# Sixteen of 22 feed-forward blocks go through the down projection as two chunks with seven products for eight

## The chip, the cores and the metric

The kernel runs on one core of one Trainium2 chip. Its engines each work through a list of instructions of their own, in order: TensorE (PE) multiplies matrices, with a separate entry PEld for its weight loads; VectorE (DVE) and ScalarE (ACT) do elementwise work; GpSimd (POOL) does a little of it; SyncE (SP) mostly issues DMA transfers between memory and the chip. An instruction that waits for another engine or for a transfer holds up everything behind it on its own engine. The metric is the device time of one execution in microseconds (us). Three runs of the kernel before gave 2496.0, 2497.52 and 2500.09 us, so the median is 2497.52 us.

## What is computed

One inference step of a hybrid decoder with one trunk layer, for a prompt of 1024 tokens and a group of 8 single-token samples, 1032 columns in all. Three token mixers (a gated convolution, a state-space scan, an attention over 256 memory tokens) read one combined input projection `w_in`; their merged output is added to `x`; then comes the feed-forward:

```python
def swiglu(xn, w_gate, w_up, w_down):
    return (jax.nn.silu(xn @ w_gate) * (xn @ w_up)) @ w_down
...
xp = xp + h
xp = xp + swiglu(rmsnorm(xp, norm_ffn_w[l]), w_ffn_gate[l], w_ffn_up[l], w_ffn_down[l])
```

`D_MODEL` is 1024 and the hidden width is 2816, so there are 22 hidden blocks of 128 (`NF`). A final RMSNorm follows. Everything is float32, and the outputs include the states of the mixers (`state_ssm` among them).

## The kernel before, in words

**Products.** Activations lie transposed, 128 features on the partitions and the 1032 tokens (`TT`) along the row. Each float32 operand is split into a high and a low part by a cast on ACT (`h`) and a subtraction on DVE (`l`), and each product is made of three: high by high, high by low, low by high.

**Plain and seven-for-eight products.** `gemm` (L194) multiplies eight or fewer blocks plainly; for a block of 128 output features and one of 128 input features it makes three matrix multiplications of 1032 columns, each issued as 256, 512 and 264 columns. `strassen` (L298) computes two output blocks from eight input blocks. It sees weights and activations as 2x2 matrices and makes seven products of half size where the plain way needs eight. The activation side of a product, its form, is a sum of token halves and feature halves: `B11`, `T1`, `nT2`, `B21`, `T3`, `B22`, `T4`. Each product runs over four pairs of 128 features with 516 columns (`HT`, issued as 256 and 260). For the weights two raw tiles are loaded (`st_raw`, L235), summed on DVE (`sa` at L323 and L324, `sb` in `st_adds2` at L289 and L290) and split into `A`, `S`, `T` and `D` tiles (`st_split`, L243 the ACT cast, L244 the DVE subtraction). Outputs are collected from three PSUM tiles in turn (`m0`, `m1`, `m2`): the first product of each quarter by an ACT copy (L326, L334, L337), the later ones by DVE additions and subtractions. The same function serves the input projection, where the blocks `Z`, `X`, `C`, `G` and `B` go through it (the first such row is at 102.71 us), and gate and up of the feed-forward (`g0` ... `g20`, `u0` ... `u20`).

**What else runs beside it.** While the input projection runs, the samples' state recurrence is interleaved with it: a tile `st` of states is loaded by SP (L831), scaled on ACT (L839), updated and read on DVE (L841, L845) and stored by SP (L853). The four `C` pairs `C0`, `C2`, `C4`, `C6` have such ACT instructions among their own casts and copies. No order is written by hand for single instructions: a scheduler lays out each engine's list when the kernel is built, from the program's order, its buffers and its dependencies; `tick` runs small pending pieces of other work between products.

**Feed-forward.** For each pair of blocks, `hidden_pair` (L1781) runs `g` and then `u`; SiLU on ACT and three multiplications on DVE (L1809, L1810, L1811) make the hidden blocks `g..o`, and SP writes them to `h_d` (L1812, L1813). After all 22 blocks the PSUM pool of `strassen` is closed and the down projection runs with `gemm` in groups of blocks 0 to 2, 3 to 10 and 11 to 18 (`down`, L1837), each added by DVE into the eight output tiles `x3_0` ... `x3_7` (L1852), which first hold the residual read from `x2_d` (L1857). `hidden` reads blocks back (`hr`, L1823) and splits them (L172, L173). Blocks 19 to 21 go through the last loop (L1913 to L1915) together with the final normalization.

## Time and profile before

| what | value |
|---|---|
| runs shown | 2496.0, 2497.52, 2500.09 us |
| the profiled execution's own time | 2499.52 us |
| its span | 2497.8 us |
| granted TensorE clock over the span | 0.995 |
| PE busy | 2446.6 us (98%) |
| DVE busy | 1504.3 us (60%) |
| ACT busy | 1047.6 us (42%) |
| DMA | 392.08 MB, mean 157 GB/s |

The profile was taken from one execution; 1.7 us of its time lie outside the span. "Busy" counts time in which an engine has an instruction in work, so PE at 98% is an engine that hardly ever waits, not one at its peak. In a row of the timeline the first two columns are start and duration in us, then engine, source line, operation, output and inputs, with the number of instructions it groups; a bracket at the end gives the idle time before it and what ended it. The names SPq and ACTq stand for the engine's DMA issues. In a table of windows each engine's busy time in the stretch stands with the number of its instructions, then the granted clock, the DMA share and the bytes per second.

### The profile page before, as it was taken

How to read it: one execution, taken by the hardware profiler on the slowest of the kernel's cores; microseconds unless marked ns; L12 is line 12 of the kernel's file. 1: busy time of each engine (PE TensorE's matmuls, PEld its weight loads, DVE VectorE, ACT ScalarE, POOL GpSimd, SP SyncE). 2: the span in 40 equal slices, each digit the busy share in tenths (PEclk: the TensorE clock that was granted, in tenths of full speed). 3: DMA queues.
4: the chain of work that ended last, by engine and by line, in shares of the span. 5: the costliest groups of instructions: out<-in, count | busy, mean ns of one | idle time of the engine just before them, and what ended most of it. 6: DMA issues, size and time to landing. Idle time of an engine off the chain costs nothing.

```text
span 2497.8 us, 44833 instructions
## 1 busy us (share of the span) xinstructions
PE 2446.6 (98%) x18714; PEld 2313.1 (93%) x18714; DVE 1504.3 (60%) x2466; ACT 1047.6 (42%) x1688; POOL 118.4 (5%) x163
## 2 busy tenths in 40 slices
PE   7999999999999999999999989999999999999998
PEld 5899999999999999888888877899999999999998
DVE  6744587777677774656767552555775545552325
ACT  6554455353545535457445441223443333341212
POOL 0200000000000001121120000000000000000000
PEclk9999999999999999999999999999999999999999
DMA  6345434344344456667868677855443222282211
GB/s 200 105 140 162 131 103 153 111 129 128 109 136 136 130 159 216 200 206 266 268 196 274 214 271 240 265 197 170 141 153 102 93 70 85 84 278 88 68 35 69
DMA packets 348330, 392.08 MB, mean 157 GB/s; under 512 B 15334, under 2 KB 285782, under 8 KB 348119
## 3 DMA queue, kind: packets, MB, share of 16 engines
q1 hardware_dynamic: 327678, 331.50, 42.4%
q10 hardware_dynamic: 20449, 57.71, 6.0%
q8 instruction: 147, 2.41, 0.4%
q14 instruction: 56, 0.46, 0.1%
HBM read 280.40 MB, written 108.98 MB: 156 GB/s over the span
## 4 chain that ended last, share of the span: by engine, by line
PE 90%; DMA 5%; DVE 3%; ACT 2%; issue 1%; SPq 0%; ACTq 0%; POOL 0%; DVEq 0%
PE po L214 12%; PE pd L214 9%; PE ps_q L214 4%; PE pm L1710 4%; PE ps_g L214 1%; PE py L953 1%; PE pss L966 1%; PE po L945 1%; PE Z4m L256 1%; PE C3m L256 1%; PE G18m L256 1%; PE B6m L256 1%; PE X14m L256 1%; PE B4m L256 1%; PE G10m L256 1%
## 5 line engine op out<-in xcount | busy, mean ns | idle before, releaser
L1852 DVE TENSOR_TENSOR x<-pd,x 128x1032 f32<-128x1032 f32 x24 | 29.5, 1231 | 128.8 <-PE pd L214 128.8
L898 ACT ACTIVATE r<-r,acum 128x128 f32<-128x128 f32 x256 | 79.3, 393 | 3.6 <-DMA r<-ac_d 3.1
L669 DVE SCALAR_TENSOR_TENSOR ax<-u,prm,ax 128x1024 f32<-128x1024 f32 x44 | 56.3, 1281 | 0.0
L930 POOL TENSOR_TENSOR xdd<-xdt,decst 128x512 f32<-128x512 f32 x32 | 38.9, 1215 | 290.0 <-DVE xdt L926 290.0
L839 ACT ACTIVATE st<-st,es 128x128 f32<-128x128 f32 x128 | 41.6, 394 | 22.4 <-DMA st<-in_state_ssm_dram 22.4
L1357 DVE TENSOR_TENSOR yr<-po,yr 128x1032 f32<-128x1032 f32 x8 | 9.8, 1231 | 56.0 <-PE po L214 45.1
L949 DVE TENSOR_TENSOR y<-po,ea 128x512 f32<-128x512 f32 x28 | 19.3, 689 | 37.2 <-PE po L945 37.2
L924 DVE TENSOR_TENSOR r<-r,cbm 128x1024 f32<-128x1024 f32 x32 | 39.2, 1225 | 2.7 <-ACT bT L923 0.5
L841 DVE SCALAR_TENSOR_TENSOR st<-sr,dts,st 128x128 f32<-128x128 f32 x128 | 40.5, 348 | 0.4
L923 ACT COPY bT<-bp 128x128 f32<-128x128 f32 x32 | 8.5, 265 | 69.9 <-DVE cbm L921 69.8
L845 DVE SCALAR_TENSOR_TENSOR sr<-st,sr 128x128 f32<-128x128 f32 x128 | 35.5, 287 | 1.1
L953 PE MATMUL py<-r,xdt 128*64 128x128 f32 x512 | 35.0, 279 | 0.0
L899 ACT ACTIVATE r<-r 128x1024 f32<-128x1024 f32 x32 | 33.9, 1058 | 0.6
L966 PE MATMUL pss<-xdd,bT 128*128 128x512 f32 x64 | 33.4, 603 | 0.0
L926 DVE TENSOR_TENSOR xdt<-xp,dtT 128x512 f32<-128x512 f32 x32 | 21.9, 685 | 18.6 <-PE xp L919 18.4
L1717 DVE TENSOR_TENSOR x<-pm,xT 128x516 f32<-128x516 f32 x16 | 11.1, 696 | 35.1 <-PE pm L1710 35.1
L953 PEld LDWEIGHTS py<-r,xdt 128*64 128x64 f32 x512 | 27.3, 137 | 4.1 <-issue 0.5
L945 PE MATMUL po<-bc,s 128*128 128x128 f32 x224 | 29.8, 276 | 1.0 <-DVE s L972 1.0
L979 POOL TENSOR_TENSOR s<-s,cdec 128x512 f32<-128x512 f32 x28 | 30.2, 1078 | 7.4 <-DVE s L972 7.0
L945 PEld LDWEIGHTS po<-bc,s 128*128 128x128 f32 x224 | 27.6, 191 | 2.8 <-issue 1.6
L1090 DVE SCALAR_TENSOR_TENSOR x<-x,prm,sqa 128x1032 f32<-128x1032 f32 x16 | 19.7, 1288 | 14.5 <-ACT sqa L1086 14.5
L672 DVE SCALAR_TENSOR_TENSOR ax<-u,prm,ax 128x1032 f32<-128x1032 f32 x22 | 28.3, 1288 | 0.0
(9105 smaller groups left out, 8780.1 us busy)
## 6 DMA issues: line engine op xcount, KB each, us to landing
r<-ac_d SPq DMA_DIRECT2D x32, 512.0 KB
gt<-gt_d SPq DMA_DIRECT2D x24, 516.0 KB
xs_d<-ax ACTq DMA_DIRECT2D x22, 516.0 KB
hr<-h_d SPq DMA_DIRECT2D x22, 516.0 KB
gt_d<-G ACTq DMA_DIRECT2D x20, 516.0 KB
x<-xs_d SPq DMA_DIRECT2D x16, 516.0 KB
zs<-zs_d SPq DMA_DIRECT2D x16, 516.0 KB
yb_d<-x SPq DMA_DIRECT2D x16, 516.0 KB
```

The lines of the kernel that those rows point to most:

```text
L214: PE.matmul(out[:, c : c + n], wt[:, ks], x[:, c : c + n], start=(k == 0 and i == 0), stop=(k == nk - 1 and i == 2),)
L256: PE.matmul(hv(ps)[:, c : c + n], wt[:, ks], x[:, c : c + n], start=(start and kt == 0 and i == 0), stop=(kt == 3 and i == 2), skip_group_ ...
L669: V.scalar_tensor_tensor(acc[:, :T], u[:, j : j + T], w[j], acc[:, :T], op0=ALU.mult, op1=ALU.add)
L839: S.activation(st[:, i], st[:, i], AF.Copy, scale=es[:, g * 4 + i, b : b + 1])
L841: V.scalar_tensor_tensor(st[:, i], rb, dts[:, g * 4 + i, b : b + 1], st[:, i], op0=ALU.mult, op1=ALU.add)
L898: S.activation(r[:, j, :], r[:, j, :], AF.Relu, scale=-1.0, bias=acum[:, c, h : h + 1])
L924: V.tensor_tensor(r, r, bc(cbm.unsqueeze(1), [P, HPG, P]), op=ALU.mult)
L930: G.tensor_tensor(b3(xdd, HPG), b3(xdt, HPG), bc(decst[:, c, hs].unsqueeze(2), [P, HPG, 64]), op=ALU.mult)
L945: PE.matmul(po[:, t * P : (t + 1) * P], state["s"][:, t * P : (t + 1) * P], bcg[1][:, cs], start=True, stop=True,)
L953: PE.matmul(py[hp : hp + 64, (h // 2) * P : (h // 2 + 1) * P], xdt[:, h * 64 : (h + 1) * 64], r[:, (h % 2) * 4 + h // 2, :], start=True, s ...
L966: PE.matmul(pss, bT, xdd, start=True, stop=True)
L1710: PE.matmul(hv(ps)[:, c : c + n], wt[:, ks], x[:, half * HT + c : half * HT + c + n], start=(k == 0 and i == 0), stop=(k == KD - 1 and i = ...
```

## The change

Hidden blocks 0 to 15 are handled in two chunks of eight. When a pair of them is ready, four more DVE operations make its share of the seven forms in float32, and SP writes seven half-width pieces to a new array `hf_d` in place of two whole blocks. After gate and up the down projection runs four `strassen` calls over chunk 0 (`d00`, `d02`, `d04`, `d06`) and four over chunk 1 (`d10` ... `d16`), each for two output blocks, with `into=True`: the first product of each quarter is added into `x3` on DVE where an ACT copy stood. The forms' SBUF tiles are those that held the forms of gate and up: `refill` calls `h_form` after a form's last product in `u20`, which loads two tiles of that form of chunk 0 and splits them on ACT and DVE; `d06` does the same for chunk 1. Blocks 16 to 18 stay with `gemm`, blocks 19 to 21 with the last loop.

In `strassen` itself, for every caller, the second weight sum is now written over the first raw tile `raw1`, and no tile `sb` is allotted.

```diff
     def st_raw(src, name):
         raw = wp.tile([P, 1024], F32, tag="raw", name=name)
+        if len(src.shape) == 4:
+            for t in range(2):
+                in_turn("raw", SY.dma_start(raw[:, t * 512 : (t + 1) * 512].rearrange("p (k c) -> p k c", k=4), src[:, t]))
+            return raw
...
-    def st_adds2(raw1, raw2, sa, nm, sums):
-        sb = sums(f"{nm}sb")
-        V.tensor_add(sb[:, :512], raw1[:, :512], raw2[:, :512])
+    def st_adds2(raw1, raw2, sa):
+        V.tensor_add(raw1[:, :512], raw1[:, :512], raw2[:, :512])
         V.scalar_tensor_tensor(
-            sb[:, 512:], sa[:, 512:], -1.0, raw1[:, 512:], op0=ALU.mult, op1=ALU.subtract
+            raw1[:, 512:], sa[:, 512:], -1.0, raw1[:, 512:], op0=ALU.mult, op1=ALU.subtract
         )
-        return sb
+        return raw1
...
+        def first(dst, ps):
+            if into:
+                V.tensor_tensor(dst, ps, dst, op=ALU.add)
+            else:
+                S.copy(dst, ps)
+        def used(f):
+            if refill is not None:
+                refill(f)
...
-            S.copy(o11, hv(pa))
+            first(o11, hv(pa))
+            used("B11")
...
+    def h_form(ch, f):
+        for i in range(2):
+            t = ev_tile(f"hf{ch}{f}{i}", (P, 2 * HT))
+            SY.dma_start(t, hf_d[ch, FORMS.index(f), i])
+            mk = fx.get(f) or act_pair
+            hi, lo = mk("ah", f"h{ch}{f}{i}h"), mk("al", f"h{ch}{f}{i}l")
+            split_to(hi, lo, t.rearrange("p (a c) -> p a c", a=2))
+            hforms[ch][f] += [(hi[:, a], lo[:, a]) for a in range(2)]
...
-        u1, u2, pa = hidden_pair("u", j)
+        u1, u2, pa = hidden_pair("u", j, (lambda f: h_form(0, f)) if j == NF - 2 else None)
...
-        SY.dma_start(h_d[j], s1)
-        SY.dma_start(h_d[j + 1], s2)
+        if j >= 16:
+            SY.dma_start(h_d[j - 16], s1)
+            SY.dma_start(h_d[j - 15], s2)
+            continue
+        b11, b12, b21, b22 = (t[:, c] for t in (s1, s2) for c in HS)
+        t1, t3, nt2, t4 = (t[:, c] for t in (u1, u2) for c in HS)
+        V.tensor_sub(t1, b12, b11)
+        V.tensor_sub(t3, b22, b12)
+        V.tensor_sub(nt2, t1, b22)
+        V.scalar_tensor_tensor(t4, nt2, -1.0, b21, op0=ALU.mult, op1=ALU.subtract)
+        kt = (j % 8) // 2
+        for f, t in enumerate((b11, t1, nt2, b21, t3, b22, t4)):
+            SY.dma_start(hf_d[j // 8, f, kt // 2][:, (kt % 2) * HT : (kt % 2 + 1) * HT], t)
...
+    for ch in range(2):
+        for m in range(0, KD, 2):
+            strassen(
+                w_rows(ch, m), w_rows(ch, m + 1), hforms[ch], f"d{ch}{m}", ev_sums,
+                lambda m=m: (x2[m][:, HS[0]], x2[m][:, HS[1]], x2[m + 1][:, HS[0]], x2[m + 1][:, HS[1]]),
+                into=True, refill=(lambda f: h_form(1, f)) if ch == 0 and m == KD - 2 else None,
+            )
...
-    js = [0, 1, 2]
-    for nxt in (range(3, 11), range(11, 19), range(19, 22)):
-        down(js, [hs.pop(j) for j in js])
-        js = list(nxt)
-        for j in js:
-            hs[j] = hidden(j)
+    js = [16, 17, 18]
+    down(js, [hs.pop(j) for j in js])
+    js = [19, 20, 21]
+    for j in js:
+        hs[j] = hidden(j)
```

The new listing shifts lines: L390 is the subtraction in `split_to` that makes a form's low part, L1850 to L1852 are the three multiplications of the pair, L248 and L247 are the two halves of `st_split`, L340 and L341 make `sa`, L293 and L294 the sum in place, L311 the ACT copy in `first`, L381 the new last subtraction into `x3`, L867 the scaling of `st`.

First place, DVE at the end of the last up pair `u20`. Before, the list holds the multiplications of the pair between splits of weights (`wd..l`) and blocks (`h..l`) for the plain down projection:

```order
L350 TENSOR_TENSOR u20o_23570<-u20o_23570,u20m_23567 128x516 [waits PE_49]
L1810 TENSOR_TENSOR g20o_23362<-g20o_23362,u20o_23570 128x516 [waits DVE_49]
L352 TENSOR_TENSOR u20o_23569<-u20o_23569,u20m_23568 128x516 [waits PE_49]
L1834 TENSOR_TENSOR wd02l<-wd01r,wd02h 128x768 [waits DMAHW3_49,Activation_49]
L1809 TENSOR_TENSOR g20o_23361<-g20o_23361,u20o_23569 128x1032 [waits DVE_49]
L1811 SCALAR_TENSOR_TENSOR g20o_23362<-u20m_23567,g20o_23362 128x516 [waits PE_49]
```

In the changed kernel (`h0...l` are the low parts of chunk 0's forms, `hf0...` their loads, `d00Al` the low part of the first weights of the first down call):

```order
L374 TENSOR_TENSOR u20o_23581<-u20o_23581,u20m_23580 128x516 [waits PE_49]
L390 TENSOR_TENSOR h0B220l<-hf0B_23811,h0B220h 128x2x516 [waits DMAHW5_49,Activation_49]
L390 TENSOR_TENSOR h0B221l<-hf0B_23817,h0B221h 128x2x516 [waits DMAHW6_49,Activation_49]
L390 TENSOR_TENSOR h0T40l<-hf0T_23851,h0T40h 128x2x516 [waits DMAHW7_49,Activation_49]
L390 TENSOR_TENSOR h0T41l<-hf0T_23857,h0T41h 128x2x516 [waits DMAHW0_49,Activation_49]
L1850 TENSOR_TENSOR g20o_23374<-g20o_23374,u20o_23581 128x1032 [waits DVE_49]
L1851 TENSOR_TENSOR g20o_23375<-g20o_23375,u20o_23582 128x516
L1852 SCALAR_TENSOR_TENSOR g20o_23375<-u20m_23579,g20o_23375 128x516 [waits PE_49]
L248 TENSOR_TENSOR d00Al<-d00r_23884,d00Ah 128x1024
L340 TENSOR_TENSOR d00sa<-d00r_23887 128x512
```

The two splits of form `T4` now stand ahead of the pair's multiplications, and `d00Al` behind all of them.

Second place, DVE between `d06`, the last call over chunk 0, and `d10`, the first over chunk 1 (new in the changed kernel):

```order
L390 TENSOR_TENSOR h1T40l<-hf1T_24775,h1T40h 128x2x516 [waits DMAHW7_49,Activation_49]
L381 TENSOR_TENSOR x_7_23882<-x_7_23882,d06m_24505 128x516 [waits PE_49]
L390 TENSOR_TENSOR h1T41l<-hf1T_24781,h1T41h 128x2x516 [waits DMAHW1_49,Activation_49]
L248 TENSOR_TENSOR d10Al<-d10r_24788,d10Ah 128x1024
L340 TENSOR_TENSOR d10sa<-d10r_24791 128x512 [waits DVE_49]
```

Again both `T4` splits stand ahead of the next call's first weights.

Third place, ACT in the input projection, in the middle of the pair `C0`. Before:

```order
L334 COPY su_4668<-C0m_4666 128x516 [waits DMAHW6_49,PE_49]
L839 ACTIVATE st_5246<-st_5246,es 128x128 x3
L243 CAST C0Dh<-C0r_4663 128x512 [waits DVE_49,PE_49]
L337 COPY c_4667<-C0m_4665 128x516 [waits PE_49]
L839 ACTIVATE st_5717<-st_5717,es 128x128 [waits DMAHW2_49,DMAHW7_49,DMAHW1_49,DVE_49]
```

and now:

```order
L311 COPY su_4656<-C0m_4654 128x516 [waits DMAHW6_49,PE_49]
L867 ACTIVATE st_5231<-st_5231,es 128x128 x2
L867 ACTIVATE st_5700<-st_5700,es 128x128 [waits DMAHW5_49,DMAHW7_49,DMAHW2_49,DVE_49]
L247 CAST C0Dh<-C0r_4651 128x512 [waits PE_49]
L311 COPY c_4655<-C0m_4653 128x516 [waits PE_49]
```

The first scaling of the next state tile, which waits for that tile's load, moved ahead of the cast `C0Dh` and of the copy that empties `C0`'s PSUM tile. The same exchange stands in `C2`, `C4` and `C6`.

More of the change, by code (lines that the diff above doesn't have):

```diff
@@ L285, in st_sums, with st_sums2, strassen @@
         return raw1, raw2, sa, st_split(sa, f"{nm}S")
-    def st_adds2(raw1, raw2, sa, nm, sums):
-        sb = sums(f"{nm}sb")
-        V.tensor_add(sb[:, :512], raw1[:, :512], raw2[:, :512])
+    def st_adds2(raw1, raw2, sa):
+        V.tensor_add(raw1[:, :512], raw1[:, :512], raw2[:, :512])
         V.scalar_tensor_tensor(
-            sb[:, 512:], sa[:, 512:], -1.0, raw1[:, 512:], op0=ALU.mult, op1=ALU.subtract
+            raw1[:, 512:], sa[:, 512:], -1.0, raw1[:, 512:], op0=ALU.mult, op1=ALU.subtract
         )
-        return sb
-    def st_sums2(*args):
-        return st_split(st_adds2(*args), f"{args[3]}T")
-    def strassen(src1, src2, forms, nm, sums, outs, early=None, after_t3=None, ready=None, hook=None):
+        return raw1
+    def st_sums2(raw1, raw2, sa, nm):
+        return st_split(st_adds2(raw1, raw2, sa), f"{nm}T")
+    def strassen(
+        src1, src2, forms, nm, sums, outs, early=None, after_t3=None, ready=None, hook=None, into=False, refill=None
+    ):
+        def first(dst, ps):
[6 more added lines that the diff above has]
+                refill(f)
         if ready is None and early is None:
@@ L325, in strassen @@
             wS = st_split(sa, f"{nm}S")
-            S.copy(o11, hv(pa))
+            first(o11, hv(pa))
+            used("B11")
         if ready is None:
-            sb = st_adds2(raw1, raw2, sa, nm, sums)
+            sb = st_adds2(raw1, raw2, sa)
         if early is None:
@@ L333, in strassen @@
         prod(pb, wS, 0, "T1", True)
-        S.copy(o22, hv(pb))
+        first(o22, hv(pb))
+        used("T1")
         prod(pa, wS, 512, "nT2", early is not None)
         if early is None:
-            S.copy(o12, hv(pa))
+            first(o12, hv(pa))
+            used("nT2")
             prod(pc, wA, 512, "B21", True)
             V.tensor_tensor(o11, hv(pc), o11, op=ALU.add)
+            used("B21")
         else:
@@ L350, in strassen @@
         V.tensor_tensor(o22, o22, hv(pa), op=ALU.subtract)
+        used("T3")
         prod(pb, wT, 512, "B22", False)
         V.tensor_tensor(o12, o12, hv(pb), op=ALU.subtract)
+        used("B22")
         tick()
@@ L355, in strassen @@
         prod(pa, wD, 0, "T4", False)
+        used("T4")
+        if into:
+            V.tensor_tensor(o21, o21, hv(pa), op=ALU.subtract)
+            return
         if early is not None:
@@ L377, in tile_kernel @@
     x2_d = dram("x2_d", [KD, P, TT])
-    h_d = dram("h_d", [NF, P, TT])
+    h_d = dram("h_d", [NF - 16, P, TT])
+    hf_d = dram("hf_d", [2, 7, 2, P, 2 * HT])
     e_d = dram("e_d", [5, P, TT])
@@ L1772, in tile_kernel @@
         form("T3", kt, b12)
-    g0 = (*g0, st_sums2(*g0[:3], "g0", ev_sums))
+    g0 = (*g0, st_sums2(*g0[:3], "g0"))
     for kt in range(4):
@@ L1779, in tile_kernel, with hidden_pair @@
         form("T4", kt, t2)
-    def hidden_pair(nm, j):
+    def hidden_pair(nm, j, refill=None):
         o = []
@@ L1797, in hidden_pair @@
             wblock(src, j * P), wblock(src, (j + 1) * P), forms, f"{nm}{j}",
-            ev_sums, outs, e, ready=g0 if (nm, j) == ("g", 0) else None,
+            ev_sums, outs, e, ready=g0 if (nm, j) == ("g", 0) else None, refill=refill,
         )
         return o[0], o[1], pa if e is None else pa
+    FORMS = ("B11", "T1", "nT2", "B21", "T3", "B22", "T4")
+    hforms = [{f: [] for f in FORMS} for _ in range(2)]
+    def h_form(ch, f):
[6 more added lines that the diff above has]
+            hforms[ch][f] += [(hi[:, a], lo[:, a]) for a in range(2)]
     hs = {}
@@ L1811, in tile_kernel, with w_rows @@
         V.scalar_tensor_tensor(s2[:, HS[0]], pa, -1.0, s2[:, HS[0]], op0=ALU.mult, op1=ALU.mult)
-        SY.dma_start(h_d[j], s1)
-        SY.dma_start(h_d[j + 1], s2)
+        if j >= 16:
[11 more added lines that the diff above has]
+            SY.dma_start(hf_d[j // 8, f, kt // 2][:, (kt % 2) * HT : (kt % 2 + 1) * HT], t)
+    def w_rows(ch, m):
+        src = a["w_ffn_down"][0, ch * 1024 : (ch + 1) * 1024, m * P : (m + 1) * P]
+        return src.rearrange("(k t p) c -> p t k c", t=2, p=P)
+    for m in range(KD):
+        x2[m] = big(f"x3_{m}")
+        SY.dma_start(x2[m], x2_d[m])
+    for ch in range(2):
[5 more added lines that the diff above has]
+            )
     st_stack.close()
@@ L1822, in hidden @@
         t = ev_tile(f"hr{j}")
-        SY.dma_start(t[:, :TT], h_d[j])
+        SY.dma_start(t[:, :TT], h_d[j - 16])
         return split_act(t[:, :TT], f"h{j}")
@@ L1852, in down @@
             V.tensor_tensor(x2[m][:, :TT], flat(ps), x2[m][:, :TT], op=ALU.add)
-    hs[0], hs[1], hs[2] = hidden(0), hidden(1), hidden(2)
-    for m in range(KD):
-        x2[m] = big(f"x3_{m}")
-        SY.dma_start(x2[m], x2_d[m])
-    js = [0, 1, 2]
-    for nxt in (range(3, 11), range(11, 19), range(19, 22)):
-        down(js, [hs.pop(j) for j in js])
-        js = list(nxt)
-        for j in js:
-            hs[j] = hidden(j)
+    for j in (16, 17, 18):
+        hs[j] = hidden(j)
[3 more added lines that the diff above has]
+    for j in js:
+        hs[j] = hidden(j)
     wd = []
```

## The prediction

> **What bounds the kernel now.** I read the page's busy times and its chain of waits first, then tables of windows over the feed-forward, then the timelines of single stages.

> ```profile
> PE 2446.6 (98%) x18714; PEld 2313.1 (93%) x18714; DVE 1504.3 (60%) x2466; ACT 1047.6 (42%) x1688; POOL 118.4 (5%) x163
> PE 90%; DMA 5%; DVE 3%; ACT 2%; issue 1%; SPq 0%; ACTq 0%; POOL 0%; DVEq 0%
> 140.00:900.00 760.00, 758.97 (x6382) 757.64 (x6381) 522.24 (x970) 360.16 (x519) 32.49 (x82) 1.00 0.43 131
> 2100.00:2200.00 100.00, 100.00 (x846) 100.00 (x844) 50.40 (x63) 33.11 (x43) 0.00 (x0) 1.00 0.30 98
> 2321.00:2421.00 100.00, 100.00 (x637) 90.58 (x636) 29.66 (x25) 16.55 (x16) 0.00 (x0) 1.00 0.19 59
> ```

> PE is busy throughout: in the input projection it idles 1.0 of 760 us, in gate and up and in the down projection not at all. So time goes only where PE gets less to do, and every new wait of PE counts in full. DVE has half its time free in gate and up, ACT two thirds.

> **Fewer products.** One seven-product call, and the plain down projection:

> ```profile
> 2081.15 0.40 PE L256 MATMUL u14m<-B110h,u14Ah 128*128 128x256 f32 x2
> 2101.08 0.40 PE L256 MATMUL g16m<-B110h,g16Ah 128*128 128x256 f32 x2
> 2220.40 0.40 PE L256 MATMUL u20m<-T42h,u20Dl 128*128 128x256 f32 x2
> 2221.68 0.71 PE L214 MATMUL pd<-h0h,wd00h 128*128 128x256 f32 x3 [0.88 <-DVE g20o L1811]
> 2222.22 0.64 PE L214 MATMUL pd<-h0l,wd00h 128*128 128x256 f32 x3
> 2437.35 0.34 PE L1913 MATMUL pl<-h19h,wl0h 128*128 128x384 f32 x1
> ```

> A call takes 2101.08 - 2081.15 = 19.93 us: 7 products x 4 feature pairs x 3 = 84 pairs of matrix multiplications, 0.237 us each, 2.85 us a product. The plain part runs from 2221.68 to 2437.35, 215.67 us for 19 blocks x 8 outputs x 3 = 456 triples, 0.473 us each. The change takes away 16 x 8 x 3 = 384 triples, 181.6 us, and puts in 8 calls, 159.4 us: **-22.1 us**. Their shapes are those of gate and up, so I take no doubt about the size beyond 0.5 us.

> **Making the forms: 0.** Eight pairs get 4 DVE operations of half width, 0.69 us each (rows of L1811 below), so 32 x 0.69 = 22 us, spread over 16 calls (about 320 us) of which DVE has half free. The writes grow from 16 blocks x 516 KB = 8.3 MB to 7 x 8 x 264 KB = 14.8 MB, 6.5 MB in 320 us or 20 GB/s, beside a DMA share of 0.30 at 98 GB/s. They stand on SP ahead of later raw loads; the raw tiles are wanted a call (19.93 us) later. Without that cover each pair would cost up to 4 x 0.69 = 2.8 us.

> **Additions into x3: 0.** In a down call the ACT copies become DVE additions; then four splits (1.23, 1.23, 1.23, 0.69 us), four sums (0.69) and nine or so evictions (0.69) make DVE some 13 of 19.93 us busy. Beyond 19.93 PE would wait for DVE.

> **Refilling the forms.** The 14 loads and splits of a chunk fit into the call before it, except form `T4`: its tiles are read until that call's last product ends, and DVE's list has both `T4` splits ahead of the next call's first weights. Prices for this:

> ```profile
> 2212.52 1.06 ACT L172 CAST h6h<-hr 128x1032 fp32r<-128x1032 f32 x1 [1.24 <-DMA hr<-h_d]
> 2209.34 1.23 DVE L173 TENSOR_TENSOR h4l<-hr,h4h 128x1032 fp32r<-128x1032 f32 x1
> 2210.49 0.69 DVE L244 TENSOR_TENSOR u20Dl<-u20r,u20Dh 128x512 fp32r<-128x512 f32 x1
> 2219.50 1.23 DVE L1809 TENSOR_TENSOR g20o<-g20o,u20o 128x1032 f32<-128x1032 f32 x1
> 2220.84 0.70 DVE L1811 SCALAR_TENSOR_TENSOR g20o<-u20m,g20o 128x516 f32<-128x516 f32 x1
> 2200.23 6.71 SPq L1823 DMA_DIRECT2D hr<-h_d  x4
> ```

> Count from the end of `u20`'s last product. The second `T4` tile's load can be issued when DVE has split `T30` and so freed a staging tile. `T3` ends 2 x 2.85 = 5.7 us before the end; a cast of 1.06 and the splits queued before it (2 x 1.15, the start-to-start distance of h4l and the next row) put the issue at about -2. For the landing there is the `hr` load of h6: the four issues end at 2206.94, its cast starts at 2212.52, 5.6 us later, with other loads behind it; that is the upper end, an estimate, and 4 us a lower one. So data at +2 to +3.6, cast 1.06, split 1.15: +4.2 to +5.8. Behind them stand the pair's three multiplications (1.15 + 0.6 + 0.6 = 2.35) and `d00Al` (1.15): +7.7 to +9.3. PE meanwhile does four pairs with the high weights, 1.0 us, and part of them late, since `d00`'s third PSUM tile is the one that the last multiplication empties. **First seam: 6.7 to 8.3 us; I take 7.8**, toward the later landing, since four `x3` loads follow on the queue, and weights `S` come late behind the same list (up to 1.8 more). From `d06` to `d10` the chain is the same without the multiplications: 7.8 - 2.35 = **5.5 us (4.4 to 6.0)**. The last seam, `d16` to the plain part, waits for the last DVE subtraction as today's does (0.88 above): **0** against today.

> **The clock after these gaps.** PE's granted clock by windows, with the wait that came before each:

> ```profile
> 133.11 1.28 PE L1196 MATMUL ps_mt<-ident,mem 128*128 128x128 f32 x6 [3.16 <-DVE meml L1201]
> 132.00:134.00 2.00, 0.89 (x6) 0.89 (x7) 1.24 (x5) 1.84 (x5) 0.00 (x0) 0.86 0.72 291
> 134.00:136.00 2.00, 2.00 (x11) 2.00 (x10) 2.00 (x2) 2.00 (x6) 0.00 (x0) 0.50 0.00 0
> 136.00:138.00 2.00, 2.00 (x15) 2.00 (x15) 1.51 (x6) 2.00 (x8) 0.00 (x0) 0.79 0.00 0
> 1440.90 0.63 PE L1557 MATMUL psp<-ident,pr 128*128 128x128 f32 x4 [2.06 <-DVE pTl L1565]
> 1442.00:1444.00 2.00, 2.00 (x15) 1.83 (x15) 2.00 (x10) 0.37 (x1) 0.00 (x0) 1.00 0.01 2
> ```

> After a gap of 3.16 us the clock is at 0.5 until about 136.8 (0.79 over two microseconds is 0.84 us at half speed); after 2.06 us it is not touched. From 133.4, when it drops (0.86 over 132 to 134 is 0.56 us at half speed), that is 3.4 us at half speed, so 1.7 us lost. Both new seams are longer than 3.16 us: **+3.4 us for two**, 0 to 6.8. [...]

> **The shared helper.** The second weight sum in place keeps the raw tile until the `T` split, so later raw loads and, with them, the scheduler's order shift in the input projection. On ACT, in `C0`, `C2`, `C4` and `C6`, the first scaling of the next state tile moved ahead of the cast `Dh` and the copy that empties the tile which product `T3` reuses. Rows of `C0`:

> ```profile
> 421.16 0.40 PE L256 MATMUL C0m<-xnh,C0Ah 128*128 128x256 f32 x2
> 429.67 0.62 ACT L243 CAST C0Dh<-C0r 128x512 fp32r<-128x512 f32 x1 [1.14 <-PE C0m L256]
> 430.20 0.58 ACT L337 COPY c<-C0m 128x516 f32<-128x516 f32 x1
> 433.65 1.28 ACT L839 ACTIVATE st<-st,es 128x128 f32<-128x128 f32 x4 [2.87 <-DMA st<-in_state_ssm_dram]
> 424.96 0.69 DVE L323 TENSOR_TENSOR C1sa<-C1r 128x512 f32<-128x512 f32 x1 [0.87 <-DMA C1r<-in_w_in_dram]
> 425.78 1.22 DVE L244 TENSOR_TENSOR C0Tl<-C0sb,C0Th 128x1024 fp32r<-128x1024 f32 x1
> 430.47 0.93 SPq L831 DMA_DIRECT2D st<-in_state_ssm_dram  x2
> ```

> `T3` is due at 421.16 + 4 x 2.85 = 432.56. Today the copy is done at 430.78. If the state lands as today, at 433.65, the scaling (0.3), the cast (0.53 to the next start) and the copy (0.58) end at 435.1: PE loses 2.5 us, or 3.4 with another load of 0.9 us ahead on the queue. Against that, DVE's list has the state update without `C1sa` and `C0Tl` in its middle (0.87 + 0.69 + 1.22 + 0.69 = 3.5 us), so the old state is stored and the new one loaded up to 3.5 us earlier than 430.47, and the wait could vanish. Four times 0 to 3.4 us; I take the middle of the plain case, a load 1 us earlier: 1.5 each, **+6 us** (0 to 13.6).

> **Sum.** -22.1 + 7.8 + 5.5 + 3.4 + 6.0 = +0.6 us on the profiled execution's 2499.52, so 2500.1. That execution stood 2.0 us above the median of the runs shown, so beside the median it is **2498 us**. About 5 us (0.2%) is what a measurement of this kernel can tell from no change. I forecast no change, 43%, its own range 2491 to 2505.

> **Rivals.**

> *State waits in full* (25%, slower). The scaling ahead of the copy decides in all four `C` pairs, the state landing no earlier than today: 4 x 3.4 = 13.6 in place of 6.0, so +8.2 us, 2506. For it: the wait for that load is the row of 2.87 us above. Against it: the 3.5 us taken out of DVE's list. It decides from about 2.6 us a pair.

> *The gate closes at small gaps as well* (8%, slower). If the `C` waits of 1.5 us also halve the clock, 4 x 1.7 = 6.8 us are added: +7.4 us, 2505. Against it stands the 2.06 us gap at 1440.90; for it, a row in a thinner stretch:

> ```profile
> 61.68 1.20 PE L214 MATMUL ps_C<-xnh,wC0h 128*128 128x256 f32 x3 [1.23 <-ACT uB L749]
> 62.00:64.00 2.00, 2.00 (x8) 1.81 (x8) 2.00 (x7) 1.99 (x3) 0.00 (x0) 0.50 0.84 240
> ```

> *Only the seams cost* (24%, faster). The state comes early enough, the seams are at their low ends and one halving at most is felt: -22.1 + 6.7 + 4.4 + 1.7 = -9.3 us, 2488. For it: the DVE list, and loads that land after 4 us. Against it, the DMA engines are nearly full at today's first seam (share 0.96):

> ```profile
> 2220.00:2222.00 2.00, 1.12 (x9) 0.94 (x9) 1.89 (x3) 0.83 (x1) 0.00 (x0) 1.00 0.96 355
> ```

> That the change doesn't do what it says, that PE doesn't get fewer products, I rule out: its list has eight calls of 84 pairs. A full gain with the seams hidden (-21 us, 2476) would need the `T4` splits behind `d00Al`, and the list has them ahead; it is in what is left out.

> **Chances and range.** No change 0.36 (of the forecast's 43, 3.5 lie beyond 5 us on either side), faster 0.28, slower 0.36. The range runs from the third rival's 2488 less its seams' last microsecond, 2487, to the first rival's 2506 with the seams' upper ends and one more halving (0.5 + 0.5 + 1.7, and 1.8 for a late `S`), 2510.

> **What would show it.** After the change: calls `d00` to `d16` at 19.9 us each, PE waits of 6 to 9 us before `d00` released by `d00Al` or the multiplication, of 4 to 6 us before `d10`, a granted clock of 0.5 for 3.4 us behind each, PE waits of 0 to 3 us at `T3` of `C0`, `C2`, `C4`, `C6` released by ACT's copy, and an input projection (140 to 900 us today) that ends that much later. I am wrong if PE idles in the middle of the down calls, if gate and up lose time to the forms, or if the input projection moves by more than 14 us in either direction.

## The result, and the profile after

The changed kernel takes 2507.46 us (median of nine runs, 2504.77 to 2511.89) beside 2499.09 us of the kernel before (nine runs, 2496.0 to 2503.3): 8.4 us more, a ratio of 1.0035 with a 95% interval of 1.0024 to 1.0045. That is slower, and clear of 0.2% at both ends of the interval. The profiled executions show the same: a span of 2505.8 us after 2497.8.

The page of the changed kernel, span and engines:

```profile
span 2505.8 us, 45588 instructions
PE 2434.5 (97%) x18906; PEld 2315.8 (92%) x18906; DVE 1596.0 (64%) x2598; ACT 1070.7 (43%) x1716; POOL 116.3 (5%) x163
```

PE is busy for 12.1 us less than before (2434.5 after 2446.6), so the fewer products are there, but the span is 8.0 us longer: PE idles 20.1 us more. The table of waits by engine says where; its columns are the total in us, the number of times and the longest:

```profile
PE d00m L260 <- DVE g20o L1852: 5.9, 1, 5.9
PE d10m L260 <- DVE x L381: 3.5, 1, 3.5
PE C6m L260 <- ACT c L311: 2.7, 1, 2.7
PE C2m L260 <- ACT c L311: 2.0, 1, 2.0
PE C0m L260 <- ACT c L311: 2.0, 1, 2.0
PE d10m L260 <- DVE d10Al L248: 2.0, 1, 2.0
PE C4m L260 <- ACT c L311: 1.5, 1, 1.5
PE u0m L260 <- DVE u0o L371: 0.9, 1, 0.9
```

None of these waits stands in the kernel before. The first, second and sixth are the two new seams (5.9 and 3.5 + 2.0 us), the four of `C` are in the input projection (8.2 us). PE's own time also got longer in places, because its granted clock was halved there (to 0.50 from 436.77 to 440.19, 866.85 to 870.26, 2235.60 to 2245.84 and 2327.76 to 2334.59 us). The windows after `C6` and around the seams (columns as before; the granted clock is the third number from the end; those of `C0` stand in the last section):

```profile
868.00:872.00 4.00, 4.00 (x27) 4.00 (x27) 1.92 (x3) 2.01 (x5) 0.00 (x0) 0.72 0.52 131
2236.00:2240.00 4.00, 0.46 (x2) 0.46 (x3) 4.00 (x5) 0.00 (x0) 0.00 (x0) 0.50 0.81 329
2240.00:2244.00 4.00, 4.00 (x19) 3.80 (x19) 3.93 (x6) 1.68 (x2) 0.00 (x0) 0.50 1.03 314
2244.00:2248.00 4.00, 4.00 (x29) 4.00 (x28) 2.24 (x3) 0.41 (x1) 0.00 (x0) 0.77 0.95 368
2328.00:2332.00 4.00, 3.25 (x15) 3.25 (x16) 3.93 (x6) 1.60 (x2) 0.00 (x0) 0.50 0.00 0
2332.00:2336.00 4.00, 4.00 (x26) 4.00 (x26) 2.32 (x3) 0.49 (x1) 0.00 (x0) 0.68 0.00 0
```

The first seam's chain, ACT and then DVE:

```profile
2234.82 1.05 ACT L389 CAST h0T41h<-hf0T 128x1032 fp32r<-128x1032 f32 x1 [1.16 <-DMA hf0T<-hf_d]
2235.90 1.23 DVE L390 TENSOR_TENSOR h0T41l<-hf0T,h0T41h 128x1032 fp32r<-128x1032 f32 x1 [0.98 <-ACT h0T41h L389]
2237.05 1.23 DVE L1850 TENSOR_TENSOR g20o<-g20o,u20o 128x1032 f32<-128x1032 f32 x1
2238.19 0.69 DVE L1851 TENSOR_TENSOR g20o<-g20o,u20o 128x516 f32<-128x516 f32 x1
2238.80 0.69 DVE L1852 SCALAR_TENSOR_TENSOR g20o<-u20m,g20o 128x516 f32<-128x516 f32 x1
2239.41 1.21 DVE L248 TENSOR_TENSOR d00Al<-d00r,d00Ah 128x1024 fp32r<-128x1024 f32 x1
```

What a seam costs as a whole is read from the starts of the down calls. PE's timeline, first products of `d00`, `d02`, `d10`, `d12`:

```profile
2232.96 0.40 PE L260 MATMUL d00m<-h0B110h,d00Ah 128*128 128x256 f32 x2
...
2262.12 0.28 PE L260 MATMUL d02m<-h0B110h,d02Ah 128*128 128x256 f32 x1
...
2321.90 0.40 PE L260 MATMUL d10m<-h1B110h,d10Ah 128*128 128x256 f32 x2
...
2350.50 0.40 PE L260 MATMUL d12m<-h1B110h,d12Ah 128*128 128x256 f32 x2
```

`d00` takes 29.16 us and `d10` 28.60, while the calls between them take the 19.93 us of gate and up ((2321.90 - 2262.12) / 3). The seams cost 9.23 and 8.67 us: waits of 5.94 and 5.49, and 3.3 and 3.2 us more in which PE ran at half clock.

Matching PE's rows of the same name in both profiles gives the sum by stage. The shift of the changed kernel against the one before:

| first row of | before | after | shift | gained by the stage before it |
|---|---|---|---|---|
| `ps_mt`, behind the wait on `meml` | 133.11 | 134.98 | +1.87 | +1.87 |
| `ps_q<-xnh,wq7h`, behind the input projection | 1085.42 | 1101.34 | +15.92 | +14.05 |
| `po<-b06l,wo30h`, behind the mixers | 1605.33 | 1616.73 | +11.40 | -4.52 |
| `u0m<-T40h,u0Dh` | 1841.27 | 1853.76 | +12.49 | +1.09 |
| `pl<-h19h`, behind the down projection | 2437.35 | 2445.42 | +8.07 | -4.42 |

The part that the change is about gained only 4.4 us. The input projection, which shares the helper, lost 14. The mixers' -4.5 us and the start's +1.9 are in code that the change doesn't touch; one piece of them is a halving of the clock (0.50 from 1140.36 to 1143.77 us) that the profile before has and this one doesn't. In the profiles of all eleven runs below, this stretch of the mixers is 1.3 to 4.9 us shorter than in this one profile of the kernel before, 4.9 where nothing but the sum in place was changed. So the -4.5 is put down to that one profile and not to the change.

### The profile page after: what moved, and what is told of

The parts are those of the page before. It is cut to its first block, busy times and chain, and to the rows that moved or that the text cites. A ratio compares the mean times of both kernels' runs of the same rounds, so it can differ in the third digit from the quotient of the medians.

```text
span 2505.8 us, 45588 instructions
## 1 busy us (share of the span) xinstructions
PE 2434.5 (97%) x18906; PEld 2315.8 (92%) x18906; DVE 1596.0 (64%) x2598; ACT 1070.7 (43%) x1716; POOL 116.3 (5%) x163
## 4 chain that ended last, share of the span: by engine, by line
PE 56%; DMA 4%; DVE 3%; ACT 1%; issue 1%; SPq 0%; ACTq 0%; DVEq 0%
PE po L214 12%; PE pm L1738 4%; PE ps_q L214 3%; PE pd L214 1%; PE py L981 1%; PE pss L994 1%; PE po L973 1%; PE d00m L260 1%; PE d10m L260 1%; PE Z14m L260 1%; PE G16m L260 1%; PE B6m L260 1%; PE C7m L260 1%; PE d16m L260 1%; PE d14m L260 1%; PE d02m L260 1%
## 5 line engine op out<-in xcount | busy, mean ns | idle before, releaser
L867 ACT ACTIVATE st<-st,es 128x128 f32<-128x128 f32 x128 | 41.6, 394 | 61.4 <-DMA st<-in_state_ssm_dram 51.5
L1950 ACT ACTIVATE fj<-psy 128x512 f32<-128x512 f32 (+1 forms) x18 | 10.7, 596 | 59.0 <-PE psy L1948 58.9
L766 ACT ACTIVATE ax<-ax 128x1032 f32<-128x1032 f32 x22 | 23.5, 1068 | 19.5 <-DVE ax L700 19.4
L1667 DVE TENSOR_TENSOR gt<-po,gt 128x1032 f32<-128x1032 f32 x8 | 9.8, 1230 | 30.0 <-PE po L214 27.8
```

The lines of the kernel that those rows point to most:

```text
L867: S.activation(st[:, i], st[:, i], AF.Copy, scale=es[:, g * 4 + i, b : b + 1])
```

## The experiments

The theory, from this account: the seams cost about 18 us of the 22 that the products save, two thirds in waits and one third in half clock, and the sum in place costs some 12 us in the input projection. Each ratio below is against the kernel before, run on the same chip; the changed kernel's is 1.0035.

**The sum in a tile of its own in the input projection.** The feed-forward keeps it in place.

```diff
+    in_place = [False]
-    def st_adds2(raw1, raw2, sa):
-        V.tensor_add(raw1[:, :512], raw1[:, :512], raw2[:, :512])
+    def st_adds2(raw1, raw2, sa, nm, sums):
+        sb = raw1 if in_place[0] else sums(f"{nm}sb")
+        V.tensor_add(sb[:, :512], raw1[:, :512], raw2[:, :512])
...
+    in_place[0] = True
     ffn = {"g": a["w_ffn_gate"][0], "u": a["w_ffn_up"][0]}
```

> The changed kernel, with the second weight sum back in a tile of its own in the input projection; the feed-forward keeps the sum in place. Theory (the sum in place moved the state's scaling ahead of a copy that the third product waits for): the waits of 2.0, 2.0, 1.5 and 2.7 us at C0, C2, C4, C6 go, and the two halvings of the clock after C0 and C6 with them, 8.2 + 3.4 = 11.6 us: 2495 to 2497, a little below the kernel before. Rival (the loss of the input projection is run-to-run or start-up, and the changed kernel is slow for the down projection alone): no more than 3 us gained, 2504 to 2508.

Measured: 2493.71 us beside 2497.54, ratio 0.9983 (0.9974 to 0.9992). The window of the input projection:

```profile
140.00:900.00 760.00, 759.08 (x6383) 757.73 (x6382) 522.38 (x968) 360.29 (x522) 32.42 (x82) 1.00 0.43 130
```

PE idles 0.9 of 760 us, as before the change (1.0). The step from 1.0035 to 0.9983 is 0.52% of 2497.5, or 13 us, a little above the 11.6 that were expected. The changed kernel without its side effect is faster than the one before by about 4 us, which is what the table by stage gave for the down projection. The rival, that the loss was not there, falls.

**The sum in place alone.** The kernel before with the other two lines as in the change:

```diff
-        sb = sums(f"{nm}sb")
+        sb = raw1
```

> The kernel before, with nothing changed but the second weight sum, which is written over the first raw tile for every caller. Theory: 10 to 13 us slower than the kernel before (2509 to 2512), with PE waits of 1.5 to 2.7 us at the third product of C0, C2, C4, C6 behind ACT's copy. Rival: within 3 us of the kernel before.

Measured: 2514.62 us beside 2497.54, ratio 1.0066 (1.0054 to 1.0079), which is 16.5 us; the expectation of 10 to 13 was too low. Its PE timeline:

```profile
436.57 0.53 PE L256 MATMUL C0m<-xnh,C0Th 128*128 128x256 f32 x2 [2.19 <-ACT c L337]
580.55 0.50 PE L256 MATMUL C2m<-xnh,C2Th 128*128 128x256 f32 x2 [1.80 <-ACT c L337]
723.24 0.50 PE L256 MATMUL C4m<-xnh,C4Th 128*128 128x256 f32 x2 [1.62 <-ACT c L337]
866.51 0.51 PE L256 MATMUL C6m<-xnh,C6Th 128*128 128x256 f32 x2 [2.65 <-ACT c L337]
...
1852.83 0.51 PE L256 MATMUL u0m<-T40h,u0Dh 128*128 128x256 f32 x2 [0.80 <-DVE u0o L350]
1868.41 0.51 PE L256 MATMUL g2m<-T40h,g2Dh 128*128 128x256 f32 x2 [0.91 <-DVE g2o L350]
1898.53 0.51 PE L256 MATMUL g4m<-T40h,g4Dh 128*128 128x256 f32 x2 [0.81 <-DVE g4o L350]
```

The same four waits are there, 8.3 us, with nothing of the down projection changed. Three waits in the first calls of gate and up, 2.5 us, were not expected; the changed kernel has one of them. With two halvings of the clock behind `C0` and `C6` (3.4 us, as in the changed kernel) the waits make 14.2 us, beside 14.0 between the two profiled spans (2511.8 after 2497.8); the rest of the 16.5 is not placed. This one edit costs more than the whole change.

**Copies first on ACT.** The sum stays in place; one ordering rule puts the first scaling of a state behind the copy of the `C` pair (no wait is taken away).

```diff
-                S.copy(dst, ps)
+                ins = S.copy(dst, ps)
+                if nm[0] == "C":
+                    c_copy[:] = [ins.ins]
...
-            S.activation(st[:, i], st[:, i], AF.Copy, scale=es[:, g * 4 + i, b : b + 1])
+            ins = S.activation(st[:, i], st[:, i], AF.Copy, scale=es[:, g * 4 + i, b : b + 1])
+            if i == 0 and n % 2 == 0 and c_copy:
+                tc.add_manual_dep(
+                    ins.ins, c_copy[0].name,
+                    mybir.DependencyInfo(mybir.DependencyClass.NoSync, mybir.DependencyReason.DATA),
+                    reason="c_copy",
+                )
```

> The changed kernel, sum in place kept, with one ordering rule more on ACT and no wait: the first scaling of a state tile comes behind the copy that empties the first tile of a C pair. Theory (the order on ACT makes the waits at C0, C2, C4, C6): they fall below 0.5 us each and the halvings of the clock after them go, 2494 to 2497 beside a kernel before of 2497.5, as with the sum in a tile of its own. Rival (the raw tile that is held longer makes them, through later loads): waits above 1 us each stay, less than 4 us gained, above 2502.

Measured: 2503.25 us beside 2496.76, ratio 1.0030 (1.0019 to 1.0042). The waits at `C0` to `C6` are gone, but its PE timeline has others:

```profile
479.47 0.50 PE L260 MATMUL B0m<-T40ah,B0Dh 128*128 128x256 f32 x2 [0.99 <-DVE b L375]
621.28 0.51 PE L260 MATMUL B2m<-T40ah,B2Dh 128*128 128x256 f32 x2 [0.84 <-DVE b L375]
763.55 0.50 PE L260 MATMUL B4m<-T40ah,B4Dh 128*128 128x256 f32 x2 [1.26 <-DVE b L375]
906.75 0.51 PE L260 MATMUL B6m<-T40ah,B6Dh 128*128 128x256 f32 x2 [2.14 <-DVE b L375]
```

5.2 us of waits moved to the `B` pairs, behind DVE. So both ideas hold a part: the order on ACT decides that `C` feels a late state, and with that order mended the time is lost elsewhere. In DVE's list the late updates of the state stand among the operations of `B0`; that they are what delays `B` was not tried. Why the state is late is read from the changed kernel's own rows, SP, DVE and ACT in `C0`:

```profile
429.76 0.38 SPq L241 DMA_DIRECT2D C1r<-in_w_in_dram  x1
430.39 0.93 SPq L859 DMA_DIRECT2D st<-in_state_ssm_dram  x2
428.51 1.22 DVE L248 TENSOR_TENSOR C0Tl<-C0r,C0Th 128x1024 fp32r<-128x1024 f32 x1
435.00 0.40 ACT L867 ACTIVATE st<-st,es 128x128 f32<-128x128 f32 x1 [5.05 <-DMA st<-in_state_ssm_dram]
435.31 0.60 ACT L247 CAST C0Dh<-C0r 128x512 fp32r<-128x512 f32 x1
435.81 0.58 ACT L311 COPY c<-C0m 128x516 f32<-128x516 f32 x1
```

DVE's split `C0Tl` ends at 429.73, and SP issues the raw load of `C1` at 429.76: with the sum in place the raw tile comes free only there. The state's load stands behind it on SP and goes out at 430.39; the scaling that waits for it starts at 435.00, 4.6 us later. In the kernel before it was 3.2 us (430.47 to 433.65), with no raw load just ahead. The times of the two profiles can't be set side by side as they are, since `C0` itself starts 1.7 us later in the changed kernel (422.87 after 421.16). Counted from each pair's first product:

| pair | load issued, before | after | issue to scaling, before | after | raw load ahead of it by, after |
|---|---|---|---|---|---|
| `C0` | 9.3 | 7.5 | 3.2 | 4.6 | 0.6 |
| `C2` | 9.4 | 7.2 | 2.8 | 5.0 | 0.5 |
| `C4` | 9.5 | 7.1 | 3.1 | 4.5 | 0.7 |
| `C6` | 9.3 | 10.1 | 2.9 | 3.0 | 2.2 |

So the load is issued about 2 us earlier in three pairs, and most of that is lost in a longer landing, where the raw load of the next block goes out just ahead of it. In the kernel with the sum in place alone the same three pairs have 4.5 to 4.9 us and `C6` 3.0. That the raw load ahead makes the landing longer fits all eight pairs, but was not tried by itself.

**T4 in the call that uses it.** The two tiles of `T4` are loaded and split behind the first product of `d00` (and `d10`), not at the end of the call before.

```diff
-        u1, u2, pa = hidden_pair("u", j, (lambda f: h_form(0, f)) if j == NF - 2 else None)
+        u1, u2, pa = hidden_pair("u", j, (lambda f: f != "T4" and h_form(0, f)) if j == NF - 2 else None)
...
+    def refills(ch, m):
+        def run(f):
+            if m == 0 and f == "B11":
+                h_form(ch, "T4")
+            if ch == 0 and m == KD - 2 and f != "T4":
+                h_form(1, f)
+        return run
...
-                into=True, refill=(lambda f: h_form(1, f)) if ch == 0 and m == KD - 2 else None,
+                into=True, refill=refills(ch, m),
```

> The changed kernel, with form T4 of each chunk loaded and split in the first down call that uses it (behind that call's first product) where it was done at the end of the call before. Theory (the two T4 splits ahead of the first weights make both seams): the PE waits before d00 and d10 fall from 5.9 and 5.5 us to 1 to 2 us each and the clock stays at full speed after them, 8 us of waits and 6 us of half clock: 2492 to 2496. Rival A (the seams wait for the refill of the forms as a whole, so the next late form takes T4's place): 3 us gained at most. Rival B (the gate does not matter): 8 us gained, 2499 to 2500.

Measured: 2501.44 us beside 2497.54, ratio 1.0015 (1.0006 to 1.0024): 5 us gained where the theory said 12 to 16. Its seams in PE's timeline:

```profile
2238.91 0.80 PE L260 MATMUL d00m<-h0B210h,d00Ah 128*128 128x256 f32 x2 [3.69 <-DVE g20o L1852]
...
2324.07 0.51 PE L260 MATMUL d10m<-h1B210h,d10Ah 128*128 128x256 f32 x2 [2.43 <-DVE x L381]
2325.21 0.52 PE L260 MATMUL d10m<-h1B110h,d10Al 128*128 128x256 f32 x2 [0.39 <-DVE d10Al L248]
```

The waits fell from 5.9 and 5.5 to 3.7 and 2.8 us, and the clock was halved once more after `d00` (its pairs of products start 0.43 us apart up to 2244.5, and 0.24 apart behind that). Rival A is nearer: `T4` was the last piece of the refill, and the forms ahead of it take its place.

**Both edits together.**

> Both edits of the two runs before in one kernel. Theory: the gains add up, 2507.5 - 11.6 - 14 = 2480 to 2485, 15 to 19 us below the kernel before, most of the 22.1 us that the fewer products are worth. Rival: the two losses hide one another or something else in the down calls costs, and it stays above 2490.

Measured: 2487.62 us beside 2497.54, ratio 0.9957 (0.9944 to 0.9971), 10.7 us faster than the kernel before. By the ratios, the two gains of 13 and 5 us against 1.0035 add up (1.0035 - 0.0052 - 0.0020 = 0.9963, inside the interval). What falls short of the expected 2480 to 2485 is the seams' edit alone.

**B22 late as well.** The same kernel, with `B22` refilled behind the first product and `T4` behind the second of the call that uses them.

```diff
+    LATE = {"B22": "B11", "T4": "T1"}
...
+            for late, at in LATE.items():
+                if m == 0 and f == at:
+                    h_form(ch, late)
+            if ch == 0 and m == KD - 2 and f not in LATE:
+                h_form(1, f)
```

> The kernel with both edits of the earlier run (sum in a tile of its own in the input projection, T4 refilled in the call that uses it), and form B22 refilled there too. Theory (any form split between the last sums and the first low weights lengthens the seam by its DVE time of 2 x 1.15 us): the waits before d00 and d10 fall from 3.6 and 1.5 us to 1 to 2 and about 1, no halving of the clock after d00, 2482 to 2485 where the kernel with both edits had 2487.6. Rival (the multiplications of the last pair hold the first seam): it stays at 2486 to 2489.

Measured: 2481.25 us beside 2496.76, ratio 0.9943 (0.9931 to 0.9956). One wait of a seam above 0.3 us is left, and the clock stays up (0.995 over the span, after 0.990 in the changed kernel):

```profile
2223.99 0.51 PE L260 MATMUL d00m<-h0B110h,d00Al 128*128 128x256 f32 x2 [1.29 <-DVE d00Al L248]
```

The medians gained 6.4 us against the run before, the ratios 3.5; their intervals overlap. In the trace the seams went from 3.6 and 1.5 us to 1.3 and under 0.3, as the theory said.

**Three forms late.** `T3` as well.

> The same with forms T3, B22 and T4 all refilled in the call that uses them. Theory: the seams as with two, 2482 to 2485; more lateness buys nothing once the clock stays up. Rival (the forms now land too late inside d00 and d10): PE waits before the T3 product of d00 or d10 of over 1 us, above 2486.

Measured: 2482.33 us beside 2496.76, ratio 0.9942 (0.9930 to 0.9955), no different from two late forms. The rival's sign is there, though not its time: PE waits 1.3 us before the `T3` product of `d10` and 0.8 us in `d00` on `h0B221l`, so forms now come late inside the calls. `d00` and `d10` together take 43.3 us after 42.0 with two late forms; the whole time doesn't show it.

**Idle products across the seams.** 20 pairs of matrix multiplications that nothing uses stand ahead of `d00` and of `d10`, first in the changed kernel:

```diff
             wA = st_split(raw1, f"{nm}A")
+            if nm in ("d00", "d10"):
+                for _ in range(20):
+                    for c, w in HALF:
+                        PE.matmul(hv(pb)[:, c : c + w], wA[0][:, :P], forms["B11"][0][0][:, c : c + w], start=True, stop=True)
             prod(pa, wA, 0, "B11", True)
```

> The changed kernel with 20 pairs of idle products (4.7 us) put on PE ahead of d00 and ahead of d10, into a PSUM tile that is overwritten later; they work out nothing that is used. Both seams still end when DVE has made the first low weights. Theory (each seam costs 2.9 to 3.2 us of half clock beyond its wait): the granted clock stays at 1.0 behind both seams and the time falls by about 6 us, to about 2500 beside a kernel before of 2497.5. Rival (the granted clock in the records is not what the time hangs on, or the idle products delay the seam): within 2 us of the changed kernel, 2505 to 2508, or slower.

Measured: 2505.15 us beside 2496.76, ratio 1.0033 (1.0021 to 1.0045): no gain in the whole time that can be told from the changed kernel's 1.0035. The clock did what was expected, at the first seam:

```profile
2236.00:2240.00 4.00, 4.00 (x37) 4.00 (x36) 2.84 (x3) 1.73 (x2) 0.00 (x0) 1.00 0.96 323
2240.00:2244.00 4.00, 1.69 (x15) 1.48 (x13) 3.59 (x5) 0.38 (x1) 0.00 (x0) 1.00 0.83 339
```

and from the row of `u0` on to `pl` it took 4.0 us less than the changed kernel (shift against before 15.84 to 7.46, where that had 12.49 to 8.07). But the stages ahead of `u0`, which the idle products don't touch, were 3.4 us slower in this execution, 2.4 of them in the mixers. And the idle products and the waits behind them take 1.1 us more at the two seams than the waits alone did (20 pairs taken as 4.7 us), since the real products that the wait used to cover, about 1.0 us, now come behind the idle ones. By the whole time this run is inconclusive, so the pair was run again on the kernel whose input projection is quiet.

> The kernel of the first run (sum in a tile of its own in the input projection, both seams as in the change), with the 20 pairs of idle products ahead of d00 and d10. Theory of the half clock: 4 to 6 us below that kernel, 2488 to 2490 beside a kernel before of 2497.5, with the granted clock at 1.0 behind both seams. Rival: no more than 2 us below it, 2492 to 2495.

> The kernel of the first run once more, beside the one with idle products on the same chip: 2493 to 2495 by either theory.

Measured on one chip: 2490.62 us with idle products (ratio 0.9962, 0.9950 to 0.9975) and 2495.1 us without (0.9981, 0.9973 to 0.9990), beside 2500.15. That is 4.7 us by the ratios; the intervals overlap by a hair (0.9973 to 0.9975). At the second seam the windows of the two show what it is, without and with:

```profile
2316.00:2320.00 4.00, 3.88 (x18) 3.88 (x19) 3.79 (x6) 2.09 (x2) 0.00 (x0) 0.50 0.00 0
```

```profile
2312.00:2316.00 4.00, 3.08 (x25) 3.07 (x26) 3.93 (x6) 1.45 (x2) 0.00 (x0) 1.00 0.01 4
```

PE issues 18 matrix multiplications in 3.88 busy us at half clock, and 25 in 3.08 at full. After `d00` the clock was halved all the same in the profiled execution (0.61 over 2225 to 2228 us), behind a rest of 2.4 us of waiting. The calls themselves gained less than the whole time: `d00` went from 29.25 to 29.08 us and `d10` from 28.45 to 26.92, 1.7 us together, while the two profiled spans are 4.3 us apart. The other 2.6 us lie ahead of `u0`, in code that is the same in both. In the first pair of kernels the two calls gained 4.0 us. So half clock has a cost of its own behind a seam, and work that computes nothing wins some of it back: 1.7 and 4.0 us in the two pairs of traces, while neither pair's whole times can be put down to it alone.

**The sum in place in the down calls alone**, on the kernel with two late forms:

```diff
-    in_place[0] = True
     ffn = {"g": a["w_ffn_gate"][0], "u": a["w_ffn_up"][0]}
...
+    in_place[0] = True
     for m in range(KD):
         x2[m] = big(f"x3_{m}")
```

> The kernel with B22 and T4 late, and the second weight sum in a tile of its own in gate and up too, so that only the down calls write it in place. Theory (the wait of 1.3 us in the first up call u0 comes from the raw tile held longer): that wait goes, about 1 us gained, 2479 to 2482. Rival: the wait stays, and the time with it.

Measured: 2479.53 us beside 2500.15, ratio 0.9916 (0.9903 to 0.9930), 21 us faster than the kernel before. The wait of `u0` is gone; from the seam on only these two waits above 0.3 us are left in the feed-forward:

```profile
2221.62 0.50 PE L260 MATMUL d00m<-h0B110h,d00Al 128*128 128x256 f32 x2 [0.82 <-DVE d00Al L248]
...
2383.78 0.71 PE L214 MATMUL pd<-h16h,wd160h 128*128 128x256 f32 x3 [0.88 <-DVE x L383]
```

It beats both kernels. In its profile the row of `pl` stands 19.5 us ahead of the one before, and 19.0 us of that are won behind `u0`: 22.1 us of products less 3.1 us that `d00`, `d02` and `d10` still take beyond 19.93 each.

## Why the prediction was right and where it was wrong

The forecast was no change, +0.6 us, with a range of 2487 to 2510 us. 2507.46 lies in the range, but the change is slower by 0.35%, which had a chance of 0.36, as much as no change. The mechanisms were the ones named; the sum was 8 us short. The range reaches 12 us above it, so the result stands inside by the width of the range and not by the sum.

- **Fewer products, -22.1 us: right.** The calls take 19.93 us each, and the kernel without the losses gained 21.
- **Making the forms and the additions, 0: right.** Gate and up run with PE at 100.00 of 100 us; DVE rose to 54 to 61%. The down calls between the seams take 19.93 us, so DVE isn't their bound.
- **First seam, 7.8 us taken, 6.7 to 8.3: 5.94 us of wait**, below the range. The order was right: `T41h` waits for its load, then `h0T41l`, the three multiplications and `d00Al`. DVE began the multiplications at 2237.05, 3.9 us behind the last product's end at 2233.13, where the working had 4.2 to 5.8. And the wait ended with the last multiplication (2239.49), which empties the PSUM tile that PE's next products write; the working counted to `d00Al` (2240.62), which those products covered. The same seam waits 7.0 and 6.9 us in the two profiles of the kernel with the sum in a tile of its own, inside the range, so one execution gives this term to about 1 us.
- **Second seam, 5.5: 5.49 us.** Right, and it ended with `d10Al` as the working had it.
- **Clock behind the seams, 3.4 us taken, 0 to 6.8: 6.5 us.** This is the largest term that was mis-sized. The step "that is 3.4 us at half speed, so 1.7 us lost" took one interval from a gap of 3.16 us. Behind the longer gaps of the seams the clock stayed halved for three and for two intervals of 3.41 us (10.24 and 6.83 us). At the first seam PE worked at half clock from 2239.5 to 2245.8, and each seam cost 3.2 to 3.3 us beyond its wait. In other profiles with the same two seams (the sum in a tile of its own, twice, and copies first on ACT) it is 2.4 to 2.7 a seam, so the term was about 5 us in those three, above the 3.4 in all four.
- **Shared helper, 6.0 us taken, 0 to 13.6: 8.2 us of waits at `C`.** The place, the releaser and the four pairs were right. "A load 1 us earlier" was not the error: from the pair's start the load was issued about 2 us earlier in three of four pairs. What failed is the landing, which the working took over from today's rows: the time from issue to scaling grew from about 3 to 4.5 to 5.0 us there, and the waits were 1.5 to 2.7 us a pair in place of 1.5. The first rival's 3.4 a pair did not come either. The input projection as a whole moved by 14.05 us, at the very edge of the 14 that were named as a sign of being wrong.
- **The second rival, 8%, came half true.** Its gate is the halving of the granted clock. The clock was halved after `C0` (a wait of 2.00 us) and `C6` (2.67), 3.41 us at 0.50 each and so 3.4 us lost together, and not after `C2` (2.01) and `C4` (1.50). The last section shows what told them apart.
- **Not seen:** the wait of 0.9 us at `u0`, from the same sum in place.

With the measured sizes the sum is -22.1 + 5.9 + 5.5 + 6.5 + 8.2 + 3.4 + 0.9 = +8.3 us, beside 8.4 between the medians. It is not proof of each part: 14.05 us were lost in the input projection by rows, 8.2 + 3.4 of them named, the start lost 1.9, and the mixers gave back 4.5 that none of these terms holds.

## What to carry to other kernels

When a faster product form needs its operands rebuilt, count what stands in the consuming engine's list between the last old product and the first new weight; the rebuild of whatever is needed last belongs behind that weight, in the call that uses it (here 10 us by the ratios, 0.9983 to 0.9943). A helper that several stages share is a change to all of them: the two lines that saved a tile cost 16.5 us alone, most of it in a stage more than 1300 us ahead of the one that they were made for. A buffer held longer moved a load, and with it the order on two other engines and what stood just ahead of the next load on the queue. And a wait of PE is priced with the half clock that was seen behind it, here 3.2 to 3.3 us beyond each seam's wait.

## What the runs showed of the hardware

```profile
433.36:436.77 3.41, 1.41 (x12) 1.21 (x11) 2.21 (x4) 1.77 (x5) 0.00 (x0) 1.00 0.50 125
436.77:440.19 3.42, 3.42 (x18) 3.42 (x17) 1.24 (x2) 2.62 (x7) 0.00 (x0) 0.50 0.61 153
576.72:580.13 3.41, 1.81 (x16) 1.60 (x14) 1.48 (x3) 1.04 (x3) 0.00 (x0) 1.00 0.70 188
580.13:583.55 3.42, 3.01 (x25) 3.01 (x26) 1.24 (x3) 3.35 (x9) 0.00 (x0) 1.00 0.42 101
```

The wait at `C0` lies wholly in one window, and PE is busy for 1.41 of its 3.41 us, 41%; the one at `C2` lies across two, and the first has 53%. With idle products it is 42% in the window of `C2` and 59% in that of `C6`. Counted over all thirteen traces between 140 and 2460 us, of the windows at full clock: in 34 PE was busy for less than 44%, and half clock followed every one; in 8 it was busy for 44 to 50%, and half clock followed three; of the 8739 above 50% it followed six, and those six hold some 2 us of matrix multiplications one column wide (`psny`), 18 of them in 2.15 us in the kernel before. In the two kernels' own profiles it followed all six below 44%, neither of the two between, and one above. So of the four waits of 1.99 to 2.58 us above, half clock followed the two that lay in one window of the grid, and not the two that lay across two. This is a count over these traces; that the busy share itself is what the hardware goes by was not tried.
